# Moving the left-hand SBUF tiles of a two-layer hybrid network by 64 bytes, and the memory's parts by 32 bytes modulo 128

## The chip, the cores and the metric

The kernel runs on one core of one Trainium2 chip. The metric is the device time of one execution in microseconds; the kernel before was run three times, with a median of 2016.8 us (2015.11 to 2018.83 us). Each run of the kernel is one launch that computes the whole network.

## The reference

The reference is a network of two layers over a sequence of 1024 positions with 1024 channels, and a memory of 256 positions. Cut to what matters:

```
mem_n = rmsnorm(mem, mem_norm_g)
# even layer
u = rmsnorm(h, g)
za, rq, rk, rv, xq, gate = split_cols(u @ w_in, EVEN_SPLITS)
y = concatenate([pool_mixer(za), retention(rq, rk, rv), mem_attention(xq, mem_n, w_mem_kv)]) * silu(gate)
h = h + y @ w_out
# odd layer
u = rmsnorm(h, g)
q, kc, vc, ks, vs, kw, vw, gl, xq, gate = split_cols(u @ w_in, ODD_SPLITS)
y = concatenate([nsa_attention(q, kc, vc, ks, vs, kw, vw, gl, ...), mem_attention(xq, mem_n, w_mem_kv)]) * silu(gate)
h = h + y @ w_out
return rmsnorm(h, final_g)
```

All of it is in float32, and a large part of the time goes into the matrix products with `w_in` and `w_out`.

## The kernel before

The 1024 positions are cut into two halves of 512 (`HT`), the channels into eight blocks of 128 partitions. A float32 product is made of three fast passes: each operand is split by `split` (ScalarE casts the high part, VectorE or GpSimd subtracts to get the low part), and `mm3` (lines 76 to 79) issues three matmuls: high by high (line 77), low of the moving operand (line 78), low of the weights (line 79). In the names of the profile the operand behind the arrow that comes first is the moving one, of 512 columns as a rule, and the second is the stationary one, a 128 by 128 block of weights; so `ps_mm<-uh,wh` moves `uh` past weights from `wh`. Each matmul has a weight load of its own.

The stages, in order of time:

- 0 to about 757 us, the even layer. `make_u` writes the normalized input as the tiles `uh`, `ul`; `gemm` multiplies them by weight tiles `wh`, `wl`. The gated results become `yh`, `yl`, and `out_proj` multiplies these by the output weights, 24 matmuls for a block of 128 channels. `pool_in` and `pool_out` use the small tiles `pfh`, `pfl`. `mem_kv` makes the memory's keys and values from the memory's parts (`mu0h` to `mu3l`), keys with the memory as the moving operand of 256 columns, values with the memory as the stationary one and the weights moving.
- About 757 to 1400 us, the projections of the odd layer. `early` and `strassen` form pairs of projections by seven products instead of eight, each a `product` of twelve matmuls. The moving operands are `B11`, `B21`, `T1`, `T2`, `T3`, `T4`, `B22`, each of four blocks with a high and a low part (`T30h` is block 0 of `T3`, high). `mem_kv` runs a second time with the parts `mv0h` to `mv3l`. The memory's attention (`mem_att`) and the compression run between the products.
- About 1400 us to the end, the attention of the odd layer: `scores` (queries `aqh`, `aql` stationary, keys `ks`, `kw` moving), `values` (probabilities `aph`, `apl` and values `vs`, `vw`, after transposes by `c_ident`), and between them `od_out`, which multiplies `yh`, `yl` by the output weights, twelve matmuls for a block.

The order of the work around the change is set by a scheduler from the program's text; the change touches none of it. SBUF is filled from two sides. Pools on the left are allocated one behind the other from the first free byte: constants (`cst`) first, then the small tiles, and then everything that lies in the left pools of the stages. Pools with `side="right"` (`wp0`, `wp` for the weights, `up` for `u`, `uoA` for `B11` and `B21`, `xp`) are allocated from the other end. So a byte added to an early constant moves everything behind it on the left side, and nothing on the right side. `mhalf` (line 115) is such a constant; it holds the exponent -0.5. `mrb` (line 537) is a scratch row of the even layer's memory stage, which lies directly ahead of the memory's parts `mu`.

Of the kernel before, what the change touches and what calls it, by code (L numbers as in the profile page):

```python
# [9 lines left out]
F32 = mybir.dt.float32  # L10
# [10 lines left out]
NMEM = 256  # L21
# [18 lines left out]
def net(tc, a, out, dbg=None):  # L40
# [4 lines left out]
    cst = ctx.enter_context(tc.tile_pool(name="cst", bufs=1))  # L45
# [17 lines left out]
    def bank(tag, shape=(128, HT)):  # L63
        if tag not in banks:
            tag = ALIAS[tag]
        return cur["ps"].tile(list(shape), F32, name="ps_" + tag, tag=tag, bufs=banks[tag])
# [45 lines left out]
    sp.dma_start(gains, a["gains"])  # L112
    ones = cst.tile([128, 128], F32, name="ones")
    dve.memset(ones, 1.0)
    mhalf = cst.tile([128, 8], F32, name="mhalf")
    dve.memset(mhalf, -0.5)
    ident = cst.tile([128, 128], F32, name="c_ident")

# [19 lines left out]
    def square_sum(ss, sq, nt, k):  # L138

        for t in range(nt):  # L140
            pe.matmul(ss[:, t:t + 1], sq[:, t * 128:(t + 1) * 128], ones[:, 0:1],
                      start=k == 0 and t == 0, stop=k == 7, skip_group_check=True)

    def rstd_col(ss, nt, keep=None):
        rs = sm.tile([128, 4], F32, name="rs")
        dve.tensor_scalar(rs[:, :nt], ss[:, :nt], 1.0 / D, EPS, OP.mult, OP.add)
        rr = cst.tile([128, 4], F32, name="rrk" + keep) if keep else sm.tile([128, 4], F32, name="rr", bufs=2)
        pool.tensor_tensor(rr[:, :nt], rs[:, :nt], mhalf[:, :nt], OP.pow)
        return rr
# [289 lines left out]
    def make_u(srcs, n, gi, pool_, tag, rr=None, xs=None):  # L439
        def load(k):  # L440
            x = up.tile([128, n], F32, name="x", tag="x", bufs=4)
            sp.dma_start(x, srcs[k])
            return x

        if rr is None:
            acc = tm2.tile([128, n], F32, name="acc", tag="acc")
            for k in range(8):
                add_square(acc, load(k), n, k == 0)
            rr = rstd_of(acc, n)
        rb = spread(rr, n, r=tm2.tile([128, n], F32, name="rb", tag="rb"))  # L450
        u = []
        for k in range(8):
            uf = xs[k] if xs else tmp.tile([128, n], F32, name="uf", tag="uf", bufs=2)
            dve.scalar_tensor_tensor(uf, xs[k] if xs else load(k), gains[:, gi, k:k + 1], rb, OP.mult, OP.mult)
            uh = pool_.tile([128, n], F32R, name="uh", tag=tag, bufs=16)
            ul = pool_.tile([128, n], F32R, name="ul", tag=tag, bufs=16)
            split(uh, ul, uf)
            u.append((uh, ul))
        return u
# [64 lines left out]
    def drain(g):  # L524
        for _ in g:
            pass

    sp.dma_start(ident, a["ident"])
    with tc.tile_pool(name="mk0", bufs=1, reuse_waits="tile") as mp_:
        xs = [mp_.tile([128, HT], F32, name=f"xs{k}") for k in range(8)]  # L530
        ss = bank("t")
        for k in range(8):
            sp.dma_start(xs[k], a["xT"][k][:, :HT])
            sq = tm2.tile([128, HT], F32, name="sqx", tag="t2", bufs=2)
            act.activation(sq, xs[k], AF.Square)
            square_sum(ss, sq, 4, k)
        mrb = mp_.tile([128, NMEM], F32, name="mrb")
        slots = [[mp_.tile([128, HT], F32R, name=f"mu{k}{x}") for x in "hl"] for k in range(4)]
        mem = mem_kv("ev", slots, mrb)
        u = make_u(None, HT, 0, up, "u", rstd_col(ss, 4), xs)  # L540
        drain(mem)
# [3 lines left out]
    if True:  # L545
# [11 lines left out]
        for hf in range(2):  # L557
# [80 lines left out]
            with ExitStack() as pc:  # L638
                pp = pc.enter_context(tc.tile_pool(name="pp", bufs=1, reuse_waits="tile"))
                mp_ = pc.enter_context(tc.tile_pool(name="mx", bufs=1, reuse_waits="tile"))  # L640
# [428 lines left out]
    with tc.tile_pool(name="mk1", bufs=1, reuse_waits="tile") as mp_:  # L1069
# [3 lines left out]
        mrb = mp_.tile([128, NMEM], F32, name="mrb1")  # L1073
# [383 lines left out]
```

## Time and profile before

| | |
|---|---|
| median of three runs | 2016.8 us (2015.11 to 2018.83) |
| the profiled execution, its own time | 2017.07 us |
| its span, first to last instruction | 2015.3 us |
| TensorE's matmuls busy | 1947.2 us, 97% of the span |
| VectorE, ScalarE, GpSimd busy | 63%, 47%, 28% |
| granted TensorE clock, mean | 0.991 |

The page gives busy time for each engine; a matmul's end is modelled, and it is counted as busy from its start to that end, so that matmuls that follow each other without a gap overlap in time. What one matmul costs in a row of them is therefore the time from its start to the start of the next one, which the timeline view shows; the duration of a single one (some 0.39 us for 512 columns) contains a constant tail on top of it. The rows are further down.

### The profile page before, as it was taken

How to read it: one execution, taken by the hardware profiler on the slowest of the kernel's cores; microseconds unless marked ns; L12 is line 12 of the kernel's file. 1: busy time of each engine (PE TensorE's matmuls, PEld its weight loads, DVE VectorE, ACT ScalarE, POOL GpSimd, SP SyncE). 2: the span in 40 equal slices, each digit the busy share in tenths (PEclk: the TensorE clock that was granted, in tenths of full speed). 3: DMA queues.
4: the chain of work that ended last, by engine and by line, in shares of the span. 5: the costliest groups of instructions: out<-in, count | busy, mean ns of one | idle time of the engine just before them, and what ended most of it. 6: DMA issues, size and time to landing. Idle time of an engine off the chain costs nothing.

```text
span 2015.3 us, 28802 instructions
## 1 busy us (share of the span) xinstructions
PE 1947.2 (97%) x9898; PEld 1621.9 (80%) x9898; DVE 1267.3 (63%) x2739; ACT 941.9 (47%) x1869; POOL 573.6 (28%) x601
## 2 busy tenths in 40 slices
PE   7999999999999999999999999997999999999997
PEld 6888888888888878787878787885888888888885
DVE  4666455655646564844449855674856677867675
ACT  4445332444432243521222434444756677667674
POOL 0120110011111000314537533333343444433422
PEclk9999999999999999999999999998999999999998
DMA  5523234442223444557645433337463532241312
GB/s 163 170 84 132 84 105 136 156 152 78 93 95 96 134 152 161 176 175 221 209 143 191 137 125 116 125 106 261 150 197 123 167 106 63 62 159 48 116 38 94
DMA packets 127959, 267.07 MB, mean 133 GB/s; under 512 B 15512, under 2 KB 32676, under 8 KB 127780
## 3 DMA queue, kind: packets, MB, share of 16 engines
q1 hardware_dynamic: 127812, 265.24, 40.6%
q8 instruction: 78, 1.28, 0.3%
q14 instruction: 69, 0.56, 0.1%
HBM read 206.44 MB, written 61.09 MB: 133 GB/s over the span
## 4 chain that ended last, share of the span: by engine, by line
PE 83%; DVE 6%; DMA 4%; POOL 2%; issue 2%; ACT 1%; SPq 0%; DVEq 0%; POOLq 0%; ACTq 0%
PE ps_mm L79 13%; PE ps_mm L77 13%; PE ps_mm L78 13%; PE ps_t L120 6%; PE ps_s L77 3%; PE ps_s L78 3%; PE ps_s L79 3%; PE ps_a L77 3%; PE ps_a L78 3%; PE ps_a L79 3%; PE ps_o L84 2%; PE ps_o L82 2%; PE ps_o L83 2%; PE ps_b L79 2%; PE ps_b L78 1%
## 5 line engine op out<-in xcount | busy, mean ns | idle before, releaser
L70 ACT CAST wh<-wr 128x512 fp32r<-128x512 f32 (+1 forms) x395 | 242.6, 618 | 476.1 <-PE ps_mm L78 303.4
L71 DVE TENSOR_TENSOR wl<-wr,wh 128x512 fp32r<-128x512 f32 (+2 forms) x295 | 219.1, 747 | 183.5 <-ACT wh L70 177.4
L77 PE MATMUL ps_mm<-uh,wh 128*128 128x512 f32 x640 | 252.4, 394 | 0.0
L79 PE MATMUL ps_mm<-uh,wl 128*128 128x512 f32 x640 | 251.9, 394 | 0.0
L78 PE MATMUL ps_mm<-ul,wh 128*128 128x512 f32 x640 | 251.4, 393 | 0.0
L77 PE MATMUL ps_mm<-yh,wh 128*128 128x512 f32 x512 | 204.9, 406 | 5.8 <-ACT wh L70 3.8
L79 PE MATMUL ps_mm<-yh,wl 128*128 128x512 f32 x512 | 205.4, 403 | 2.0 <-DVE wl L71 1.3
L78 PE MATMUL ps_mm<-yl,wh 128*128 128x512 f32 x512 | 206.2, 403 | 0.0
L71 POOL TENSOR_TENSOR wl<-wr,wh 128x512 fp32r<-128x512 f32 x100 | 134.5, 1347 | 205.1 <-ACT wh L70 157.7
L71 DVE TENSOR_TENSOR apl<-ps_t,aph 128x512 fp32r<-128x512 f32 x204 | 136.2, 671 | 44.4 <-ACT aph L70 34.6
L70 ACT CAST aph<-ps_t 128x512 fp32r<-128x512 f32 x204 | 115.0, 568 | 84.6 <-PE ps_o L83 42.2
L1225 POOL TENSOR_TENSOR Pw<-Pw,arc 128x640 f32<-128x640 f32 (+2 forms) x96 | 96.3, 1004 | 158.3 <-DVE arc L1221 87.6
L79 PEld LDWEIGHTS ps_mm<-uh,wl 128*128 128x128 f32 x640 | 120.2, 188 | 24.4
L78 PEld LDWEIGHTS ps_mm<-ul,wh 128*128 128x128 f32 x640 | 120.2, 188 | 24.0
L77 PEld LDWEIGHTS ps_mm<-uh,wh 128*128 128x128 f32 x640 | 120.3, 188 | 23.8
L77 PEld LDWEIGHTS ps_mm<-yh,wh 128*128 128x128 f32 x512 | 95.9, 189 | 28.1 <-ACT wh L70 6.5
L70 ACT CAST wh<-ws 128x512 fp32r<-128x512 f32 x88 | 53.8, 618 | 135.8 <-PE ps_a L78 45.3
L79 PEld LDWEIGHTS ps_mm<-yh,wl 128*128 128x128 f32 x512 | 96.8, 189 | 23.7 <-DVE wl L71 2.4
L78 PEld LDWEIGHTS ps_mm<-yl,wh 128*128 128x128 f32 x512 | 96.9, 189 | 20.8 <-issue 0.8
L71 DVE TENSOR_TENSOR wl<-ws,wh 128x512 fp32r<-128x512 f32 x88 | 78.2, 896 | 56.3 <-ACT wh L70 53.2
L1217 ACT ACTIVATE Ps<-Ps,anm 128x512 f32<-128x512 f32 (+3 forms) x96 | 74.6, 777 | 26.2 <-DVE anm L1214 25.7
L1227 ACT ACTIVATE Ps<-Ps,arc 128x512 f32<-128x512 f32 (+3 forms) x96 | 74.7, 778 | 20.6 <-DVE arc L1221 18.7
(997 smaller groups left out, 4808.3 us busy)
## 6 DMA issues: line engine op xcount, KB each, us to landing
wr<-in_ev_gate SPq DMA_DIRECT2D x32, 512.0 KB, 3.5
wr<-in_ev_out SPq DMA_DIRECT2D x32, 512.0 KB, 3.6
wr<-in_od_out SPq DMA_DIRECT2D x64, 256.0 KB, 3.0
oa<-oho SPq DMA_DIRECT2D x52, 256.0 KB, 2.0
oxr<-oa SPq DMA_DIRECT2D x52, 256.0 KB, 2.9
wr<-in_od_q SPq DMA_DIRECT2D x16, 512.0 KB, 3.6
w<-in_cmp_w SPq DMA_DIRECT2D x16, 512.0 KB, 4.6
wr<-in_od_gate SPq DMA_DIRECT2D x16, 512.0 KB, 4.0
```

The lines of the kernel that those rows point to most:

```text
L70: act.copy(hi, src)
L71: (eng or dve).tensor_tensor(lo, src, hi.bitcast(F32), OP.subtract)
L77: pe.matmul(o, wh, xh, start=start, stop=False, skip_group_check=skip)
L78: pe.matmul(o, wh, xl, start=False, stop=False, skip_group_check=skip)
L79: pe.matmul(o, wl, xh, start=False, stop=stop, skip_group_check=skip)
L82: pe.matmul(o, wh, xh, start=start, stop=False)
L83: pe.matmul(o, wl, xh, start=False, stop=False)
L84: pe.matmul(o, wh, xl, start=False, stop=stop)
L120: pe.transpose(o, x, ident[:k, :k])
L1217: act.activation(pt, pt, AF.Exp, bias=nm[:, bi:bi + 1], accum_out=su[:, bi:bi + 1])
L1225: pool.tensor_tensor(pt, pt, rc[:, bi:bi + 1].to_broadcast(list(pt.shape)), OP.mult)
L1227: act.activation(pt, pt, AF.Copy, scale=rc[:, bi:bi + 1])
```

## The change

Two tiles become larger; the added elements are not read by anything that follows.

```diff
@@ -112,7 +112,7 @@
-    mhalf = cst.tile([128, 8], F32, name="mhalf")
+    mhalf = cst.tile([128, 24], F32, name="mhalf")
     dve.memset(mhalf, -0.5)
@@ -534,7 +534,7 @@
-        mrb = mp_.tile([128, NMEM], F32, name="mrb")
+        mrb = mp_.tile([128, NMEM + 24], F32, name="mrb")[:, :NMEM]
```

`mhalf` grows by 16 elements, 64 bytes in each partition, and so every tile behind it on the left side begins 64 bytes further. `mrb` grows by 24 elements, 96 bytes, and so the even layer's memory parts `mu` begin 160 bytes further in all, which is 32 modulo 128. The instructions of all engines and their order stay as they are; one instruction is larger, the memset of `mhalf`, of 24 columns in place of 8.

Where operands of matmuls begin in a partition, modulo 128 bytes, as the two built programs place them:

| tiles | side | before | after |
|---|---|---|---|
| weights `wh`, `wl` | right | 96 | 96 |
| `uh`, `ul`; `B11`, `B21` | right | 96 | 96 |
| `yh`, `yl`; `pfh`, `pfl`; `T1` to `T4`; `B22` | left | 32 | 96 |
| memory's parts of the even layer, `mu` | left | 64 | 96 |
| memory's parts of the odd layer, `mv0h` to `mv3l` | left | 32 | 96 |
| `mk`, `mv` (keys and values), `xqh`, `xql`, `mph`, `mpl` | left | 32 | 96 |
| attention: `aqh`, `aql`, `ks`, `kw`, `vs`, `vw`, `aph`, `apl` | left | 32 | 96 |
| `c_ident` and most tiles that are transposed | left | 32 | 96 |
| compression: `kp`, `w` | left | 96 | 32 |

The weight slices inside `wh` and `wl` are 512 bytes apart, so they keep the remainder.

## Rows read from the trace of the kernel before

**Rows 1.** The page: busy us, share of the span and instructions of four engines, and the chain of work that ended last, its shares by engine.

```profile
PE 1947.2 (97%) x9898; PEld 1621.9 (80%) x9898; DVE 1267.3 (63%) x2739; ACT 941.9 (47%) x1869; POOL 573.6 (28%) x601
PE 83%; DVE 6%; DMA 4%; POOL 2%; issue 2%; ACT 1%; SPq 0%; DVEq 0%; POOLq 0%; ACTq 0%
```

**Rows 2.** The waits of TensorE alone, longest in total first: what waited, for whom, us in total, times, longest one.

```profile
PE ps_t L120 <- DMA vraw<-ovs: 10.6, 3, 10.1
PE ps_t L141 <- ACT sqx L535: 7.8, 3, 5.6
PE ps_t L161 <- DVE dg L156: 4.1, 2, 2.3
...
PE ps_mm L77 <- ACT wh L70: 3.8, 3, 2.1
```

**Rows 3.** The tile views of `uh`, `yh`, `pfh`, `B210h`, `T11h` and `B220h`, the matmuls that move them past weights: count, duration in ns (smallest, median, largest), first and last start in us. `uh` and `pfh` belong to the even layer, `yh` to both layers, the last three to the odd layer's projections.

```profile
L77 PE MATMUL ps_mm<-uh,wh x640: 387/389/537, 62.1 to 734.7; 128*128 128x512 f32 x160
...
L77 PE MATMUL ps_mm<-yh,wh x512: 387/394/794, 272.7 to 1998.1; 128*128 128x512 f32 x171
...
L77 PE MATMUL ps_mm<-pfh,wh x28: 394/394/398, 89.4 to 522.4; 128*128 128x512 f32 x28
...
L77 PE MATMUL ps_c<-B210h,wh x16: 387/389/500, 812.6 to 1348.2; 128*128 128x512 f32 x16
...
L77 PE MATMUL ps_b<-T11h,wh x22: 388/394/398, 843.6 to 1362.0; 128*128 128x512 f32 x22
...
L77 PE MATMUL ps_b<-B220h,wh x22: 388/394/478, 852.4 to 1366.9; 128*128 128x512 f32 x22
```

**Rows 4.** The timeline of TensorE's matmuls in one unbroken stretch of the even layer, where `u` against weights goes over into `pf` against weights: start in us, duration. From the first to the third row there are 29 matmuls, from the fourth to the last 14.

```profile
149.45 0.39 PE L77 MATMUL ps_mm<-uh,wh 128*128 128x512 f32 x1
149.68 0.39 PE L78 MATMUL ps_mm<-ul,wh 128*128 128x512 f32 x1
...
156.03 0.39 PE L79 MATMUL ps_mm<-uh,wl 128*128 128x512 f32 x1
156.25 0.39 PE L77 MATMUL ps_mm<-pfh,wh 128*128 128x512 f32 x1
...
159.52 0.40 PE L79 MATMUL ps_mm<-pfh,wl 128*128 128x512 f32 x1
```

**Rows 5.** The timeline of the weight loads in the same stretch: start in us, duration.

```profile
150.13 0.19 PEld L78 LDWEIGHTS ps_mm<-ul,wh 128*128 128x128 f32 x1
150.36 0.19 PEld L79 LDWEIGHTS ps_mm<-uh,wl 128*128 128x128 f32 x1
```

**Rows 6.** The timeline of TensorE in the attention, a stretch in which seven matmuls of 512 columns follow each other, all with both operands on the left side. From the first to the last row there are six starts.

```profile
1441.73 0.39 PE L78 MATMUL ps_s<-kw0l,aqh 128*128 128x512 f32 x1
1441.96 0.39 PE L79 MATMUL ps_s<-kw0h,aql 128*128 128x512 f32 x1
1442.19 0.39 PE L84 MATMUL ps_o<-apl,vs0h 128*128 128x512 f32 x1
...
1443.10 0.33 PE L77 MATMUL ps_s<-ks0h,aqh 128*128 128x384 f32 x1
```

**Rows 7.** The timeline of TensorE where a run of `u` against weights begins behind a run of `pf` against weights.

```profile
95.69 0.40 PE L77 MATMUL ps_mm<-uh,wh 128*128 128x512 f32 x1
95.92 0.40 PE L78 MATMUL ps_mm<-ul,wh 128*128 128x512 f32 x1
96.16 0.39 PE L79 MATMUL ps_mm<-uh,wl 128*128 128x512 f32 x1
96.39 0.39 PE L77 MATMUL ps_mm<-uh,wh 128*128 128x512 f32 x1
...
97.06 0.39 PE L77 MATMUL ps_mm<-uh,wh 128*128 128x512 f32 x1
```

**Rows 8.** The tile views of `mv0h` (a part of the odd layer's memory, moving with 256 columns against weights, and standing still while weights move with 512) and of `mk` (keys, moving with 256 columns against the queries), columns as in rows 3.

```profile
L77 PE MATMUL ps_s<-mv0h,wh x4: 276/276/281, 860.8 to 874.6; 128*128 128x256 f32 x4
L77 PE MATMUL ps_s<-wh,mv0h x2: 396/396/396, 891.1 to 891.4; 128*128 128x512 f32 x2
...
L77 PE MATMUL ps_s<-mk,xqh x64: 278/283/287, 92.9 to 1341.4; 128*128 128x256 f32 x64
```

**Rows 9.** Groups by line and shape on ScalarE and VectorE: count, busy us, mean ns of one, idle time before and its releasers. In the first and third row both SBUF operands lie on the right side, in the second and fourth on the left.

```profile
L70 ACT CAST wh<-wr 128x512 fp32r<-128x512 f32 x390 | 240.1, 620 | 470.6 <-PE ps_mm L78 302.8 <-PE ps_a L78 50.5 <-issue 26.9
...
L70 ACT CAST yh<-yf 128x512 fp32r<-128x512 f32 x56 | 34.3, 619 | 36.3 <-DVE yf L521 31.8 <-DVE yf L392 3.1 <-PE ps_mm L78 1.2
...
L71 DVE TENSOR_TENSOR wl<-wr,wh 128x512 fp32r<-128x512 f32 x290 | 214.8, 745 | 183.5 <-ACT wh L70 177.4 <-PE ps_t L120 4.7
...
L71 DVE TENSOR_TENSOR yl<-yf,yh 128x512 fp32r<-128x512 f32 x56 | 40.5, 729 | 9.9 <-ACT yh L70 9.8
```

**Rows 10.** The tile views of `mhalf` (its memset), of `c_ident` and of `aqh`, the last two with short matmuls with both operands on the left side, columns as in rows 3.

```profile
L116 DVE MEMSET mhalf<- x1: 65/65/65, 0.9 to 0.9; 128x8 f32 x1
...
L120 PE MATMUL ps_t<-c_ident,Ps x432: 270/272/331, 1420.6 to 1971.2; 128*128 128x128 f32 x144
...
L77 PE MATMUL ps_s<-kw0h,aqh x72: 220/338/478, 1392.5 to 1783.3; 128*128 128x384 f32 x30, 128*128 128x256 f32 x30, 128*128 128x512 f32 x6, 128*128 128x128 f32 x6
```

## The prediction

> **What bounds the kernel now.** I read the page first. TensorE is busy for 97% of the span, and the chain of work that ended last lies on it for 83%; no other engine has more than 63% [rows 1]. Then its waits: the longest in total is 10.6 us (one transfer of 10.1 us at the change from projections to attention), the next 7.8 us, and an ordinary wait for weights makes 3.8 us [rows 2]; the whole list adds up to 58.6 us, under 3% of the span. So what counts is how fast matmuls follow each other where nothing is waited for. Then the tile views, to see whether like matmuls cost alike, and they don't: 512 columns against a full block of weights take 389 ns at the median for `uh` and `B210h`, and 394 ns for `yh`, `pfh`, `T11h` and `B220h` [rows 3]. `B210h` and `B220h` run in one stage against the same weight tiles, so it isn't the stage. The timeline gives the pace without the modelled tail: 29 starts of `u` from 149.45 to 156.03 us are 226.9 ns apart, and the 14 of `pf` that follow without a gap, from 156.25 to 159.52 us, 233.6 ns [rows 4]. What differs is where the operands begin modulo 128: `uh` and `B21` at 96 like the weights, the four others at 32. The weight load of the next matmul starts with the running one and takes 0.19 us of its 0.23 [rows 5], so both operands are read at the same time for most of every matmul.
>
> **Is it the address, the side, or the difference?** `u` and the weights lie on the right, the slower ones on the left, so the side would explain rows 4 as well. Against it stands a stretch of the attention in which both operands are on the left, both at 32: six starts from 1441.73 to 1443.10 us, 228.3 ns apart [rows 6], which is 227 to 229 within the rounding of the two ends. Equal remainders give the fast pace there too. I take the difference of the two remainders as the cause, for 512 columns.
>
> **The change part by part.** No instruction changes its place, on any engine or queue; no wait and no transfer is added or taken away.
>
> (a) *The memset of `mhalf`* has 24 columns in place of 8. It took 65 ns at 0.9 us [rows 10], while the first loads are on their way. Three times that, 0.2 us, is the most it could cost; I take 0.
>
> (b) *The left operands against weights.* `yh`, `yl` make 3 x 512 = 1,536 matmuls, `T1` to `T4` 16 blocks x 3 x 22 = 1,056, `B22` 4 x 3 x 22 = 264, `pf` 3 x 28 = 84 [rows 3]: 2,940, all with unequal remainders now and equal ones (96 and 96) after. If each gained the whole 6.7 ns of rows 4, it would be 19.7 us, the upper bound of this part. But the fast pace needs a run: behind a run of `pf`, the first three matmuls of `u` start 0.23, 0.24 and 0.23 us apart, and only from 96.39 us on it is 0.67 us for three [rows 7]. So I went through the starts of all of them, from 89.4 to 1998.6 us [rows 3]: in 221 the next start is over 271 ns away (a wait, or a change of shape), where I count nothing; 2,078 of the others will stand at least three places into an unbroken run of 512-column matmuls with equal remainders, and 644 won't. Over the trace, matmuls with equal remainders at 96 are 227.2 ns apart from the third place of a run on, and 231.7 before it; those of unequal ones 233.4 and 232.8. So 2,078 x 6.2 = 12.9 us, and 644 x 1.1 = 0.7 us. By stage that is about a third in the even layer, half in the projections, and a sixth in the attention, where runs are short.
>
> (c) *The memory's parts.* Where weights move past them, 512 columns, `mv0h` has 396 ns now [rows 8]; 93 such matmuls, with `mu`, at 6 ns are 0.6 us. Where they move themselves, 256 columns, the remainders 32 and 96 of `mv0h` go well together: 276 ns, against 283 for `mk` and `xqh`, both at 32 [rows 8]. By the difference, the 96 matmuls of `mv` will lose that: 96 x 6 = 0.6 us. For `mu` (64 against 96 now) no undisturbed row shows a price; the bounds are those 0.6 us to either side, and I take 0.
>
> (d) *Pairs that lie on the left together* (attention, memory attention, transposes) move together and keep their difference; I take 0. The bounds come in the rivals.
>
> (e) *The other engines.* ScalarE's cast takes 620 ns on right-hand tiles at 96 and 619 on left-hand ones; VectorE's subtraction 745 and 729 [rows 9]. I see no price of the place, and take 0.
>
> The sum: 12.9 + 0.7 + 0.6 - 0.6 = 13.6 us of TensorE time. Not all of it reaches the end. What is late next is the weights: the cast of a weight tile and its subtraction, which TensorE waits for a little already [rows 2]. The chain's 83% on TensorE is the lower bound of what passes (11.3 us), all of it the upper one. I take 94%, nearer to the upper end since the list of waits is short: 12.8 us. The profiled execution took 2017.1 us, which gives 2004.3; the median of the three runs lies 0.3 us below that execution, so **2004.0 us** is the prediction.
>
> **The rivals.**
>
> *The place itself counts, 96 being better than 32.* Then short left-hand pairs gain as well: 660 matmuls of 256 columns, 468 of 384 and 639 of 512 on the left with both at 32, of which rows 10 and 6 show some. At 5 ns each, some 1,500 undisturbed ones would give 7.5 us on top: **1996.5 us**. For it: `mk` at 283 against `mv0h` at 276 [rows 8]. Against it: rows 6, fast with both at 32.
>
> *Nothing happens, 2016.8 us.* It would be so if the pace hung on the side after all, or on which tiles share a run. For it: the fast rows 4 are all right-hand pairs, and rows 6 are one short stretch. Against it: the same rows 6. The Trainium skill (TensorE: Matmul & The Clock Gate, Step-by-step: what each phase is for) says that TensorE has two independent read ports, one for the moving operand and one for weight loads, so that loading the next weights takes no bandwidth from the running matmul. By that rule where operands begin could not matter, and the change would be worth nothing; the trace speaks against it, with 226.9 and 233.6 ns for like matmuls in one stretch.
>
> *Slower.* Equal remainders at 96 might be good for a long stream and bad for a short one: a matmul of 256 columns is best with unequal ones [rows 8], and no row shows a short pair with both at 96. The transposes (1,176 with both at 32; `Ps` alone 432 at 272 ns) and the 1,380 short matmuls of the attention and the memory's heads [rows 10] would pay one step of 6.7 ns: 2,556 x 6.7 = 17.1 us. Against the gain of 12.8 that makes **2021.1 us**; it decides from 5.0 ns a matmul on. Against it: short pairs at 32 already pay about that step (283 against 276), and nothing sets 96 apart from 32 in rows 4 and 6.
>
> **How the numbers follow.** The forecast, faster by 7 to 16 us, has 0.72. The place itself 0.10, nothing 0.11, slower 0.07. The range: the forecast's bounds (11.3 to 13.6 us of gain, with 2 us for the spread of the runs) give 2001 to 2008; I extend it below to the first rival at 1996, and above to 2010, half of the gain, since the share of settled runs is the least certain factor; that holds 0.82. A measurement of this kernel can tell about 0.2%, 4 us. Faster by more than that: the forecast and the first rival, 0.82; within it 0.12; slower 0.06, the last rival less a little that comes out even.
>
> **What would show it.** In the tile views after: medians of 389 ns for `yh`, `pfh`, `T11h` and `B220h` in place of 394; a pace of 227 ns on both sides of the border of rows 4; `mv0h` against weights at 282 in place of 276; `mk` and the transposes as before, 283 and 272; ScalarE and VectorE as in rows 9. If the medians fall and the time doesn't, waits for `wh` and `wl` have grown. If `mk` falls to 276 it is the place. If `yh` stays at 394, the reading of rows 6 was wrong.

## The result, and the profile after

The changed kernel takes 2006.55 us (median of four runs, 2005.38 to 2007.2), the kernel before 2017.55 us beside it (four runs, 2015.11 to 2018.83): a ratio of 0.9946 with a 95% interval of 0.9929 to 0.9964. A second measurement with more runs, among the experiments, gave 2004.85 us and 0.9939 (0.9927 to 0.9952). It is faster, by 11 to 12 us; the forecast of 2004.0 us is a ratio of 0.9937. The profiled execution took 2006.08 us, its span is 2004.3 us, 11.0 us shorter than before, at a mean granted clock of 0.986 (before 0.991).

The page after, busy us of the engines and the chain, the answer to [rows 1]:

```profile
PE 1939.9 (97%) x9898; PEld 1629.3 (81%) x9898; DVE 1269.6 (63%) x2739; ACT 941.8 (47%) x1869; POOL 572.9 (29%) x601
...
PE 84%; DVE 6%; DMA 4%; issue 2%; POOL 2%; ACT 1%; SPq 0%; DVEq 0%; POOLq 0%; ACTq 0%
```

The instruction counts are the same on every engine and the chain lies where it lay. TensorE's busy time falls by only 7.3 us, since matmuls that overlap are counted once; the gain must be read from starts. TensorE's waits after, columns as in [rows 2]:

```profile
PE ps_t L120 <- DMA vraw<-ovs: 10.3, 2, 9.6
PE ps_t L141 <- ACT sqx L535: 8.0, 3, 5.9
...
PE ps_mm L77 <- ACT wh L70: 3.5, 2, 2.1
```

No wait has grown into the place of the time saved: the whole list is 54.8 us where it was 58.6. Now the tile views after, columns as in [rows 3] and [rows 8]; the last row answers to the one of `c_ident` in [rows 10]:

```profile
L77 PE MATMUL ps_mm<-uh,wh x640: 387/389/532, 63.1 to 732.2; 128*128 128x512 f32 x160
...
L77 PE MATMUL ps_mm<-yh,wh x512: 387/389/796, 273.3 to 1987.2; 128*128 128x512 f32 x171
...
L77 PE MATMUL ps_mm<-pfh,wh x28: 389/389/396, 90.4 to 520.8; 128*128 128x512 f32 x28
...
L77 PE MATMUL ps_c<-B210h,wh x16: 389/389/500, 809.0 to 1338.2; 128*128 128x512 f32 x16
...
L77 PE MATMUL ps_b<-T11h,wh x22: 388/389/397, 840.7 to 1351.7; 128*128 128x512 f32 x22
...
L77 PE MATMUL ps_b<-B220h,wh x22: 388/389/476, 849.7 to 1356.5; 128*128 128x512 f32 x22
...
L77 PE MATMUL ps_s<-mv0h,wh x4: 278/283/283, 857.9 to 872.0; 128*128 128x256 f32 x4
...
L77 PE MATMUL ps_s<-wh,mv0h x2: 389/389/389, 887.1 to 887.4; 128*128 128x512 f32 x2
...
L77 PE MATMUL ps_s<-mk,xqh x64: 274/283/283, 93.8 to 1331.4; 128*128 128x256 f32 x64
...
L120 PE MATMUL ps_t<-c_ident,Ps x432: 270/272/421, 1409.7 to 1959.5; 128*128 128x128 f32 x144
```

All medians of 394 have become 389, `mv0h` has changed both ways as forecast (396 to 389 where weights move past it, 276 to 283 where it moves), and `mk` and the transposes stand where they stood. The timeline of TensorE's matmuls after, at the border of [rows 4]: start in us, duration.

```profile
149.58 0.39 PE L77 MATMUL ps_mm<-uh,wh 128*128 128x512 f32 x1
...
157.06 0.39 PE L77 MATMUL ps_mm<-pfh,wh 128*128 128x512 f32 x1
...
160.23 0.39 PE L79 MATMUL ps_mm<-pfh,wl 128*128 128x512 f32 x1
```

Between the first two rows lie 33 starts, 226.7 ns apart; between the last two 14, 226.4 ns apart, where [rows 4] have 233.6. The border is gone.

To see what passed to the end I set the two traces side by side matmul by matmul, from each start to the next start; both programs issue the same 9,898 matmuls in the same order. The left operands against weights, forecast at 13.6 us, are 4.8 ns faster in the mean where nothing disturbs them, that is, where the next start is at most 271 ns away (233.2 ns in 2,719 of them, now 228.4 in 2,704), which makes 13.0 us; with their waits and changes of clock they give 11.4. What is missing there has a place, in stretches in which TensorE's granted clock is at the lower of its two levels. The windows of the trace after, TensorE alone: stretch, us, busy us and matmuls, granted clock, share of the DMA engines, GB/s.

```profile
1732.00:1740.30 8.30, 6.48 (x40) 1.00 0.01 3
1740.30:1743.70 3.40, 3.40 (x13) 0.50 0.64 184
1743.70:1748.00 4.30, 4.30 (x21) 1.00 0.65 210
1960.00:1969.00 9.00, 7.57 (x43) 1.00 0.00 0
1969.00:1972.40 3.40, 3.38 (x9) 0.50 0.42 106
1972.40:1980.00 7.60, 7.60 (x35) 1.00 0.61 192
```

For 3.4 us at 1740.3 and at 1969.0 the clock is 0.50, 1.2 GHz, with TensorE busy all the time; ahead of each TensorE was busy for 78 and 84% of some 8 or 9 us. The same instructions ran at 1.00 before. Twelve starts from 1740.47 to 1743.80 us take 3.33 us, and 1.79 before; seven from 1969.33 us take 3.22, and 2.40 before. Two more such stretches, at 835.7 and 941.5 us, cost 1.3 and 1.6 us in the same way. Together that is 5.3 us, against 3.8 us by which the waits are shorter. One that both traces have, at 914.2 us now, lasts 6.8 us in place of 3.4 and costs another 1.6 us.

The stretches are not the same in every execution: in the profile of the second measurement (2002.73 us) those at 1740, 1969 and 941 us don't occur, while those at 836 and 914 do. They don't need the gain either. At the same matmuls as 941 and 1740 the clock falls with the left side 32 bytes further, at those of 836 and 914 with 96 bytes, at those of 836 and 1969 with 192 bytes; these are three kernels of the experiments that gain nothing. Nor did TensorE do anything else ahead of the places of 1740 and 1969 in the trace of before: there too it was busy for 78 and 84% (6.58 of 8.40 us from 1744.2, 7.47 of 8.90 from 1971.7), and the clock stayed at 1.00. The trace of before has the least time at 0.50 of all twelve profiles, 39.2 us; the others have 48.7 to 61.4.

### The profile page after: what moved, and what is told of

Read it like the earlier page. It is cut to its first block, busy times and chain, and to the rows that moved or that the text cites. A ratio compares the mean times of both kernels' runs of the same rounds, so it can differ in the third digit from the quotient of the medians.

```text
span 2004.3 us, 28802 instructions
## 1 busy us (share of the span) xinstructions
PE 1939.9 (97%) x9898; PEld 1629.3 (81%) x9898; DVE 1269.6 (63%) x2739; ACT 941.8 (47%) x1869; POOL 572.9 (29%) x601
## 4 chain that ended last, share of the span: by engine, by line
PE 84%; DVE 6%; DMA 4%; issue 2%; POOL 2%; ACT 1%; SPq 0%; DVEq 0%; POOLq 0%; ACTq 0%
PE ps_mm L79 13%; PE ps_mm L77 13%; PE ps_mm L78 13%; PE ps_t L120 6%; PE ps_s L77 3%; PE ps_s L78 3%; PE ps_s L79 3%; PE ps_a L77 3%; PE ps_a L78 3%; PE ps_a L79 3%; PE ps_o L84 2%; PE ps_o L82 2%; PE ps_o L83 2%; PE ps_b L79 2%; PE ps_b L78 2%
```

## The experiments

Nine kernels other than the two, and the changed one again. Unless the text says otherwise, all keep every instruction of every engine in its place, and only addresses and the length of the memset of `mhalf` differ. "Pace" is the mean time from start to start of left operands of 512 columns against weights, undisturbed, over the whole trace. All ratios are against the kernel before, timed beside the kernel.

**Equal remainders somewhere else.** The kernel before, with the right side moved by 64 bytes instead of the left one: weights, `u` and the left operands all begin at 32 modulo 128. `mhalf` moves into a pool of its own on the right, 64 bytes long, and `ones` takes over its 32 bytes on the left, so that the left side stays where it was.

```diff
-    ones = cst.tile([128, 128], F32, name="ones")
+    ones = cst.tile([128, 136], F32, name="ones")[:, :128]
-    mhalf = cst.tile([128, 8], F32, name="mhalf")
+    mhalf = ctx.enter_context(tc.tile_pool(name="cstr", bufs=1, side="right")).tile([128, 16], F32, name="mhalf")
```

> The kernel before with the right-hand side moved by 64 bytes in place of the left-hand one: weights, u, B11 and B21 at 32 modulo 128, the left at 32 as before (the even layer's memory parts at 64). Theory 1, the difference of the two remainders decides for 512 columns: yh, pfh, T11h, B220h and uh all at a median of 389 ns, mv0h against weights at 283, time as after the change, 2005 to 2008 us, ratio about 0.995. Theory 2, the place 96 is what is fast: uh and B210h rise from 389 to 394 as well, some 2,454 matmuls by 6 ns, 2030 to 2033 us. Theory 3, only right-hand pairs are fast: uh 389, yh 394, 2016 to 2019 us.

2004.43 us (2003.06 to 2005.82), ratio 0.9942 (0.993 to 0.9954): the whole gain. The timeline of TensorE, the run of `pf` behind `u`, 14 starts:

```profile
155.45 0.39 PE L77 MATMUL ps_mm<-pfh,wh 128*128 128x512 f32 x1
...
158.62 0.39 PE L79 MATMUL ps_mm<-pfh,wl 128*128 128x512 f32 x1
```

226.4 ns, and 228.5 over the whole trace. The value 96 has no merit, and the side has none: what counts is how the two operands stand to each other.

**Left operands 128 bytes further.** By my reading (modulo 128) this is the kernel before.

```diff
-    mhalf = cst.tile([128, 8], F32, name="mhalf")
+    mhalf = cst.tile([128, 40], F32, name="mhalf")
```

> The kernel before with the left side moved by 128 bytes, remainders as before. Theories 1 and 2: no change, 2016 to 2019 us, yh at 394 ns. A theory by which any move of the left side helps (other bits of the address, other neighbours): 2005 to 2008 us.

2009.96 us (2006.3 to 2011.44), ratio 0.9966 (0.9954 to 0.9979). No theory on record had that. The timeline of TensorE in the same run of `pf`:

```profile
156.06 0.40 PE L77 MATMUL ps_mm<-pfh,wh 128*128 128x512 f32 x1
...
159.28 0.40 PE L79 MATMUL ps_mm<-pfh,wl 128*128 128x512 f32 x1
```

14 starts in 3.22 us are 230.0 ns, halfway between the paces of [rows 4]. So 128 bytes are not a period of it. Modulo 256 the left operands began at 160 before and the weights at 224, 64 apart on one side; here they are at 32, which is 64 ahead on the other.

**Two other distances.** `mhalf` with 16 columns puts the left operands 32 bytes further, with 32 columns 96 bytes further.

```diff
-    mhalf = cst.tile([128, 8], F32, name="mhalf")
+    mhalf = cst.tile([128, 16], F32, name="mhalf")
```

> The left side moved by 32 bytes: left at 64, weights at 96, a difference of 32; the even layer's memory parts at 96. Theory 1 as I have it (only equal remainders are fast): yh, T11h, B220h at 394 ns, 2015 to 2019 us. If a smaller difference is better by degrees: 391 to 392 ns and some 2012 us. If the remainder modulo 32 were what counts, 389 ns and 2006 us.

```diff
-    mhalf = cst.tile([128, 8], F32, name="mhalf")
+    mhalf = cst.tile([128, 32], F32, name="mhalf")
```

> The left side moved by 96 bytes: left at 0, weights at 96, a difference of 32 the other way round; the even layer's memory parts at 32. Theory 1: yh, T11h, B220h at 394 ns, 2015 to 2019 us. If a start on a 128-byte border helped by itself: below 394 ns also for the left-hand pairs, mk under 283, and below 2012 us.

2016.78 us, ratio 0.9998 (0.9989 to 1.0006), and 2015.88 us, ratio 1.0001 (0.9992 to 1.0009). The same run of `pf` in the first of them, and then in the second:

```profile
155.83 0.40 PE L77 MATMUL ps_mm<-pfh,wh 128*128 128x512 f32 x1
...
159.10 0.40 PE L79 MATMUL ps_mm<-pfh,wl 128*128 128x512 f32 x1
```

```profile
155.66 0.40 PE L77 MATMUL ps_mm<-pfh,wh 128*128 128x512 f32 x1
...
158.93 0.40 PE L79 MATMUL ps_mm<-pfh,wl 128*128 128x512 f32 x1
```

Both 3.27 us for 14 starts, 233.6 ns: 32 bytes off to either side gives nothing. The gain is not a matter of degree.

**Equal modulo 128, unequal modulo 256.** The test that the last three asked for: left operands 192 bytes further, at 96 modulo 128 as in the change, but 128 bytes from the weights modulo 256.

```diff
-    mhalf = cst.tile([128, 8], F32, name="mhalf")
+    mhalf = cst.tile([128, 56], F32, name="mhalf")
```

> The kernel before with the left side moved by 192 bytes (mhalf of 56 columns): left and right at the same remainder modulo 128, 96, but 128 bytes apart modulo 256. Theory 1 as predicted, equal remainders modulo 128 are enough: yh, T11h, B220h at 389 ns and 2004 to 2008 us, as after the change. Theory 4, made after move128, whose left side lies 64 ahead of the weights modulo 256 and was faster than before (192 ahead): the difference counts modulo 256, and 128 is a third case; then T11h is not at 389 but between 391 and 396 ns, and the time between 2009 and 2018 us.

2016.19 us (2013.46 to 2018.77), ratio 0.9993 (0.9984 to 1.0002). The same run of `pf`:

```profile
155.51 0.40 PE L77 MATMUL ps_mm<-pfh,wh 128*128 128x512 f32 x1
...
158.77 0.39 PE L79 MATMUL ps_mm<-pfh,wl 128*128 128x512 f32 x1
```

3.26 us, 232.9 ns. By the rule of the prediction, equal remainders modulo 128, this kernel should be as fast as the changed one, and it isn't faster than the kernel before. The equality must hold modulo 256. The change fulfils that too: its 64 bytes take the left operands from 160 to 224, where the weights are. A period of 512 or 1024 is excluded by the changed kernel itself: there the differences modulo 1024 are 0, 256, 512 and 768, over 1,200 undisturbed matmuls each, and their paces 227.8, 228.3, 227.8 and 228.6 ns.

**Only the low parts of the weights.** The changed kernel with every `wl` 64 bytes further, so that a third of the matmuls (line 79) have unequal remainders. Here the order of a few waits of the other engines differs.

```diff
-        l = cur["wp"].tile([128, HT], F32R, name="wl", tag="wl", bufs=cur["wh"])
+        l = cur["wp"].tile([128, HT + 64], F32R, name="wl", tag="wl", bufs=cur["wh"])[:, 16:16 + HT]
```

> The kernel after the change with the low weight tiles wl moved 64 bytes further, all else equal: high weights and moving operands at the same remainder modulo 256, low weights 64 ahead. Which weights must fit the moving operand? Line 77 and 78 use wh, line 79 uses wl; while line 78 runs, the weights of line 79 are being loaded. If the weights that are being loaded count (both operands are read at the same time), line 78 becomes slow, starts some 233 ns apart, and lines 77 and 79 stay at 227. If a matmul's own weights count, line 79 is slow and line 78 stays. Either way a third of some 5,400 matmuls by up to 6 ns: 2010 to 2016 us.

2017.17 us (2015.55 to 2019.44), ratio 1.0 (0.9991 to 1.0009), above the 2010 to 2016 us expected: the whole gain is lost, and `u`, which was fast in the kernel before, pays as much as the left operands do. The tile views of `uh` and `ul`:

```profile
L77 PE MATMUL ps_mm<-uh,wh x640: 389/389/532, 61.6 to 738.4; 128*128 128x512 f32 x160
...
L79 PE MATMUL ps_mm<-uh,wl x640: 389/397/529, 62.1 to 738.8; 128*128 128x512 f32 x160
...
L78 PE MATMUL ps_mm<-ul,wh x640: 387/392/534, 61.8 to 738.6; 128*128 128x512 f32 x160
```

In the changed kernel all three have 389. Start to start, `u` takes 229.0, 229.3 and 234.7 ns on lines 77, 78 and 79, where the changed kernel has 227.7 to 227.9. So most of the loss is line 79's, over `u` and the left operands alike; lines 77 and 78 keep most of their pace. If it were the weights being loaded for the next matmul that count, line 78, during which `wl` is loaded, would be the slow one; it is line 79, whose own weights are the displaced ones, and the other two pay 1 to 2 ns as well. Which reads meet there is not settled by this.

**Half of the change.** `mhalf` grows, `mrb` doesn't, so the even layer's memory parts stay unequal to the weights.

```diff
-    mhalf = cst.tile([128, 8], F32, name="mhalf")
+    mhalf = cst.tile([128, 24], F32, name="mhalf")
```

> The first half of the change alone: mhalf of 24 columns, mrb as before, so the even layer's memory parts lie at 0 in place of 96. Every theory: the time of the changed kernel to within its spread, 2004 to 2008 us; only the 48 matmuls that move weights past mu differ, some 394 ns in place of 389, 0.3 us.

2005.12 us in one run. The tile view of `mu0h` in it, weights moving past it, and then the same row of the changed kernel:

```profile
L77 PE MATMUL ps_s<-wh,mu0h x2: 398/398/399, 51.0 to 53.3; 128*128 128x512 f32 x2
```

```profile
L77 PE MATMUL ps_s<-wh,mu0h x2: 389/392/396, 51.2 to 53.5; 128*128 128x512 f32 x2
```

The pace of all 512-column matmuls past `mu` is 233.9 ns, and 228.3 in the changed kernel; times half of the 93 that is 0.3 us, too little to see in the time. As far as one run can show, all that can be measured of the change is in the 64 bytes of `mhalf`.

**Short matmuls with unequal remainders.** The changed kernel with the attention's keys 64 bytes ahead of the queries modulo 256, the probabilities ahead of the values, and the queries of the memory's heads ahead of the keys. It was made because [rows 8] show 256 columns faster with unequal remainders.

```diff
-        qh = p_.tile([128, HT], F32R, name="xqh", tag="xqh", bufs=bufs)
-        ql = p_.tile([128, HT], F32R, name="xql", tag="xql", bufs=bufs)
+        qh = p_.tile([128, HT + 16], F32R, name="xqh", tag="xqh", bufs=bufs)[:, 16:]
+        ql = p_.tile([128, HT + 48], F32R, name="xql", tag="xql", bufs=bufs)[:, :HT]
...
+            n = {"ks0h": 16, "vs0h": 32, "vw1l": 16}
```

> The kernel after the change with three things moved against their partners by 64 bytes modulo 256: the keys of the attention 64 ahead of the queries, the probabilities 64 ahead of the values, and the queries of the memory's heads 64 ahead of their keys. All else as after. If a difference of 64 helps a matmul of 256 columns wherever it runs: mk and xqh fall from 283 to 276 ns (192 matmuls, 1.1 us), the 256-column matmuls of the attention by 5 ns (2.3 us), 512-column ones rise by at most 3 ns (1.5 us): 1 to 3 us below the changed kernel. If short runs in the attention have no settled pace, only the memory's heads gain, 1 us, within the noise of the time and visible in the tile views alone.

2004.34 us, ratio 0.9937 (0.9924 to 0.9949), beside 0.9939 of the changed kernel timed with it: no difference. The tile view of `mk`:

```profile
L77 PE MATMUL ps_s<-mk,xqh x64: 277/281/282, 91.9 to 1328.9; 128*128 128x256 f32 x64
```

281 ns, not 276. Start to start, undisturbed, 256 columns of the attentions went from 118.9 ns in the changed kernel to 117.8, 384 from 175.5 to 174.5, and 512 columns of the odd layer's attention rose from 231.0 to 231.8. Placement has little hold on these short, mixed runs.

**The changed kernel again**, as the neighbour of these:

> The changed kernel once more, beside m192 and short64 on the same chip: 2004 to 2008 us. It says also whether the stretches of low granted clock (57.8 us in all in its first profile, 39.2 in that of the kernel before) come at the same places again.

2004.85 us (2002.73 to 2006.67) beside 2018.05, ratio 0.9939 (0.9927 to 0.9952).

**Memory parts of the odd layer as with 128 bytes.** The changed kernel with `mv` 64 bytes further, at the very address at which the kernel with 128 bytes had 113.4 ns for their 256 columns.

```diff
-        mrb = mp_.tile([128, NMEM], F32, name="mrb1")
+        mrb = mp_.tile([128, NMEM + 16], F32, name="mrb1")[:, :NMEM]
```

> The kernel after the change with mrb1 16 columns larger, so that the odd layer's memory parts lie 64 bytes further, 64 ahead of the weights modulo 256. mv0h against weights, 256 columns: back from 283 to 276 ns, 0.6 us for 96 matmuls. Weights past mv0h, 512 columns: from 389 back to 394 or more, 0.3 us for 48. The time can't tell it: 2002 to 2008 us.

2004.18 us in one run. The tile view of `mv0h` in the kernel with 128 bytes, moving, and then in this one:

```profile
L77 PE MATMUL ps_s<-mv0h,wh x4: 276/277/277, 859.9 to 873.5; 128*128 128x256 f32 x4
```

```profile
L77 PE MATMUL ps_s<-mv0h,wh x4: 279/279/282, 855.1 to 869.1; 128*128 128x256 f32 x4
...
L77 PE MATMUL ps_s<-wh,mv0h x2: 393/396/398, 884.6 to 884.9; 128*128 128x512 f32 x2
```

Where weights move past it, the loss is there (396). Where it moves, the pace is 117.8 ns: better than the 119.7 of the changed kernel, but not 113.4. The same address doesn't give the same pace for 256 columns; what else goes into it stays open.

The pace of 512 columns by where the moving operand begins, seen from the weights:

| bytes ahead, modulo 256 | kernel | pace, ns | ratio of the time |
|---|---|---|---|
| 0 | the change; weights moved instead | 228.4; 228.5 | 0.9946, 0.9939; 0.9942 |
| 32 | left side 96 further | 233.0 | 1.0001 |
| 64 | left side 128 further | 230.0 | 0.9966 |
| 128 | left side 192 further | 232.5 | 0.9993 |
| 192 | the kernel before | 233.2 | 1 |
| 224 | left side 32 further | 233.0 | 0.9998 |

## Why the prediction was right

**What bounds the kernel.** Right: matmuls that wait for nothing became faster, and the end moved with them, with no other engine or transfer in between.

**The address, the side, or the difference.** Right on the difference: the kernel with all operands at 32 has the whole gain, which settles it against the side and against the value. Wrong on the modulus. The step "What differs is where the operands begin modulo 128" fitted the rows that the prediction shows of the trace of before, since there the fast pairs are also equal modulo 256 (`u` and weights both at 224, the pairs of [rows 6] all at 160) and the slow ones unequal in both. The forecast came out because the change makes both equal. That is luck as far as the rule goes: 192 bytes fulfil it as well and gave nothing where it would have forecast the same 2004 us, and 128 bytes gave 7 us where it would have forecast none.

**(b), the left operands.** Right in mechanism, the modulus apart, and in size: 13.6 us forecast, 13.0 measured where undisturbed. That the first matmuls of a run gain less was a needed part, and it holds: in the changed kernel all 512-column matmuls against weights are 227.6 ns apart from the third place of a run on, and 232.6 before it. At the full 6.7 ns of [rows 4] the 2,940 would have made 19.7 us. The counts of the forecast hold three matmuls too many (2,078, 644 and 221 make 2,943), worth 0.02 us.

**(c), the memory's parts.** Right: the 256 columns of `mv` lost 0.60 us (113.5 to 119.7 ns, 96 times), and weights past `mu` and `mv` gained 5.6 ns each (233.9 to 228.3 and 232.3 to 226.7), 0.5 us in all; the keys of `mu` changed by 0.05 us. The reason given, that remainders of 32 and 96 go well together for 256 columns, did not hold up as a rule: with 128 bytes `mv` has such remainders and 277 ns, but at the same address in the last kernel it has 279, and `mk` at such a distance from its queries has 281.

**(a), (d) and (e).** The pairs on the left side gave 1.5 us in four classes (0.37 for 256 columns, 0.69 for 384, 0.18 for 512, 0.27 for transposes), between the 0 that I took and the 7.5 of the rival, with waits and clock in it. For 96 of them the record shows what it is: the memory attention's 512-column matmuls (`mph`, `mpl` past `mv`) go from 232.9 to 227.1 ns, though their two operands begin equal modulo 256 in both kernels. With weights and `u` moved in place of the left side they have 227.2, at their own addresses of before. So they gain with the matmuls around them, 0.5 us that step (d) put at nothing. The other engines show no price of the place: ScalarE's cast takes 620 ns on right-hand tiles and 618 on left-hand ones, VectorE's subtraction 748 and 729, as in [rows 9]. The memset costs 13 ns more; the tile view of `mhalf` after, columns as in [rows 10]:

```profile
L116 DVE MEMSET mhalf<- x1: 78/78/78, 1.0 to 1.0; 128x24 f32 x1
```

**What passes to the end.** 94% was forecast; 11.0 of 13.6 us are 81%, and the second measurement, with 0.61% of 2018 us, is 12.3 us or 90%. The share came out near enough, but for a reason that isn't the one given. What the prediction named as late next was the weights [rows 2], and the wait for them fell from 3.8 to 3.5 us; what took time back was the granted clock, as the windows show. A part of that is chance, since the trace of before has the least of it. A part goes with the gain: the mean granted clock is 0.986 over nine runs of the changed kernel and 0.988 over fifteen of the kernel before, 0.987 with everything at 32, and 0.988 where 32, 96 or 192 bytes gave nothing. From these means I estimate 8 us more at the lower level (0.002 of 2005 us, at half the clock), at most some 4 us of time. Why the faster kernels have more of it stays open.

**The rivals.** The place itself is out by the kernel with everything at 32. That nothing happens is out by the time. The Trainium skill (TensorE: Matmul & The Clock Gate, Step-by-step: what each phase is for) states the rule behind that rival: two independent read ports, so that loading weights takes no bandwidth from the running matmul. That rule does not show why like matmuls should take 226.4 ns at one distance and 233.6 at another; whether it is the loading that costs them is not shown here. Slower by the short pairs is out: transposes 272 ns, `mk` 283, both unchanged.

## What to carry to other kernels

Where TensorE runs long chains of 512-column float32 matmuls with a new block of weights for each, compare the addresses at which the moving operand and the weights begin modulo 256, for all passes, low weights included; here equal ones were worth 5 ns a matmul and 0.6% of the kernel, for 64 bytes of padding in one tile. Read the addresses from the built program after every change of a tile ahead of them, since one scratch row moves everything behind it. And before a rule is taken from a trace, look for a second rule that fits the same rows: modulo 128 and modulo 256 could not be told apart until a kernel was made for it.

## What was not expected of the hardware

- The distance counts modulo 256, and not smoothly: 0 gives 228.4 ns, 32 to either side 233.0, but 64 ahead 230.0, while 64 behind is the slow kernel before (233.2).
- Displacing only the low weights by 64 bytes cost 12 us, as much as the change gains (2017.17 us): line 79 is slow for `u` too, and lines 77 and 78, whose own weights lie right, pay 1 to 2 ns each.
- 256 columns have a pace of 113.4, 117.8 or 119.7 ns for the same shape, and the address alone doesn't decide which.
- Two executions of the same changed kernel differ in where the granted clock falls to 0.50 for 3.4 us, and each such stretch costs 0.8 to 1.6 us here. The same places come and go in kernels with and without the gain.
- Matmuls whose own operands kept their addresses became 6 ns faster when those around them did (`mph`, `mpl` past `mv`, 232.9 to 227.2 ns, with everything at 32).
